# A two-layer token-mixing backbone on one core: the second layer's modulation and sums of weights loaded into slots a step ahead, and its first attention blocks placed in other slots

## The chip, the cores and the metric

The kernel runs on one core of one Trainium2 chip. The metric is the device time of one launch, in microseconds (us). Three runs of the kernel before gave 1685.3, 1686.6 and 1686.74 us; their median is 1686.6 us.

## What is computed

The reference is a backbone of two layers over 512 latent tokens (the stream X) and 256 context tokens (the stream C), 1024 channels wide. Cut to what matters here:

```python
def trunk_layer(x, ctx, c, c_ctx, ..., update_ctx):
    sh_a, sc_a, g_a, sh_f, sc_f, g_f = split(silu(c) @ w_mod + b_mod, 6)          # for x; the same with c_ctx for ctx
    zx = modulate(rms_norm(x, norm_g[0]), sh_a, sc_a) @ w_in
    zc = modulate(rms_norm(ctx, norm_g[0]), csh_a, csc_a) @ w_in
    mix_x, mix_c = token_mixers(zx, zc, ...)   # gating | mLSTM | attention | pooling, side by side
    x = x + g_a * rms_norm(mix_x @ w_out, norm_g[1])
    x = x + g_f * rms_norm(swiglu(modulate(rms_norm(x, norm_g[2]), sh_f, sc_f), w_ffn_in, w_ffn_out), norm_g[3])
    if update_ctx: ...                          # the same for ctx, in the first layer only
    return x, ctx

for l in range(2):
    x, ctx = trunk_layer(x, ctx, ..., w_mod[l], ..., update_ctx=l < 1)
return x
```

The modulation of a layer is `silu(c) @ w_mod`: a vector of 1024 times a matrix of 1024 x 6144. Everything is float32.

## The kernel before

**Products.** A float32 product is made of three TensorE matmuls of a shorter format (`mac3`, lines 491 to 493): high part times high part, low times high, high times low. Each tile of weights comes by DMA from the SP queue into a ring `wr` of seven 512 KB buffers (`weights`, L433), ACT writes its high part `wh` (L416), and DVE or POOL the low part `wl` (L417).

**Background tasks.** Each call of `weights` first calls `tick`. It adds `bg_rate` to a counter and, for each whole number that it reaches, takes a task out of the list `bg`; a second list `bg2` has a rate of its own. So work that is needed later is spread over the program of a stage. What is still in `bg` when its result is needed is issued in one go by `flush`.

**The two kinds of task of this case.** `mods_sums` makes four of the six parts of the second layer's modulation for X on DVE: 4 parts x 2 halves x 4 pairs of row blocks, 32 tasks. A task loads 512 KB of `w_mod` into one buffer of the ring `wr` (L688) and adds two scaled row blocks into an accumulator `macc` (L696 the first, L698 the others). After four tasks TensorE sums `macc` over the partitions (L704, eight small matmuls by two groups, x8 in the rows) and DVE adds the bias into `mod` (L708). `weight_sums` makes, for a Strassen form of the second layer's FFN, sums of weights: 9 tasks, each with two loads and a scratch buffer in the ring `wr`, four additions on POOL (L1566) and three stores to a DRAM tensor `ws` (L1589 to L1591). Both kinds are queued when the first layer's FFN for X begins. `bg_rate` there is 0.2, as set for an earlier stage (`rate1`).

**The first layer's end.** `layer_end` runs the output projection and then the FFN in three chunks (`fcx`); in the last one the columns are treated in two halves, so that the residual and the next norm of one half run while TensorE works on the other. In its helper the remaining tasks of `bg` are flushed (L1888 and L1891) before the second layer's projection, whose right side `hx` needs `mod`.

**Slots.** Intermediate tiles live in an `Arena` of named SBUF slots with a list of free ones, first in, first out. A tile that takes a slot waits for the last reader of what stood there.

**The second layer.** A string, `l1`, gives the order in which the pieces of the second layer's projection, mLSTM (`m`), attention (`a`), pooling (`P`) and gating (`S`) are written out; a scheduler keeps that order as the priority on every engine. `h` gives back 16 slots of `hx` after the projection; `a1` is one attention block with four heads: scores (L1115 to L1128), their exponentials into slots `pb` (L1135, the context part) and `pa` (L1140, the local part), transposes (L1162, L1168) and products. An mLSTM step ends with a norm on DVE that writes `ht` (L821), which TensorE transposes (L1452).

Of the kernel before, what the change touches and what calls it, by code (L numbers as in the profile page):

```python
# [11 lines left out]
F32 = mybir.dt.float32  # L12
# [5 lines left out]
ALU = mybir.AluOpType  # L18
# [3 lines left out]
P = 128  # L22
# [58 lines left out]
 'op1': 'P',  # L81
 'urg': 1500,
 'l0': 'k u2 q Q A B K F o u2 p2 p2 h a1 a1 S a2 a1 a2 a2 a2 P a1 a1 C N a2 R G m1',
 'l1': 'H Q R G o m2 m1 B m2 m2 m9 K u1 m2 u2 p1 p2 p2 p2 u1 u1 u1 p1 u9 p1 u1 p2 p2 p2 p2 p9 u1 h a1 m1 P a1 S a1 a1 a1 a9 a2 a1',
 'rc': 'x',
 'r0': 'x',
 'r1': 'm',
# [39 lines left out]
UNIT = 1024  # L127
# [31 lines left out]
class Arena:  # L159
# [109 lines left out]
class Build:  # L269
# [193 lines left out]
    def tick(self):  # L463
# [216 lines left out]
    def mods_sums(self, l, parts, p, streams):  # L680

        nc = self.nc
        p.mod = getattr(p, "mod", None) or self.pp.tile([P, 48, 2], F32, tag=f"mod{l}", name=f"mod{l}")

        def pair(part, i, k0, acc):
            raw = self.wr.tile([P, UNIT], F32, tag="wr", name=self.name("wr"))
            c = slice(i * 512, i * 512 + 512)
            nc.sync.dma_start(out=raw.rearrange("p (k c) -> p k c", k=2), in_=self.I["wmod"][l, part, k0:k0 + 2, :, c].rearrange("k p c -> p k c"))  # L688
            if k0 == 0:
                acc += [self.main.get("macc") for _ in range(streams)]  # L690
            for k in (k0, k0 + 1):
                w = raw[:, (k - k0) * 512:(k - k0) * 512 + 512]
                for s in range(streams):
                    t = acc[s].t[:, 0:512]
                    if k == 0:
                        nc.vector.tensor_scalar(out=t, in0=w, scalar1=self.cs[:, k, s:s + 1], scalar2=1.0, op0=ALU.mult, op1=ALU.mult)  # L696
                    else:
                        nc.vector.scalar_tensor_tensor(out=t, in0=w, scalar=self.cs[:, k, s:s + 1], in1=t, op0=ALU.mult, op1=ALU.add)  # L698
            if k0 < KT - 2:
                return  # L700
            ps = self.ms()
            for s in range(streams):
                for b in range(4):
                    nc.tensor.matmul(ps[:, s * 4 + b:s * 4 + b + 1], acc[s].t[:, b * P:(b + 1) * P], self.ones[:, 0:1], start=True, stop=True)  # L704
                acc[s].free()
            o = part * 8 + i * 4
            for s in range(streams):
                nc.vector.tensor_tensor(out=p.mod[:, o:o + 4, s], in0=ps[:, s * 4:s * 4 + 4], in1=p.bmod[:, o:o + 4], op=ALU.add)  # L708

        for part in parts:  # L710
            for i in range(2):
                acc = []
                for k0 in range(0, KT, 2):
                    self.bg.append(lambda part=part, i=i, k0=k0, acc=acc: pair(part, i, k0, acc))

    def mod_col(self, p, l, s, kind):

# [862 lines left out]
    def weight_sums(self, l, js):  # L1580

        nc = self.nc

        def task(j):
# [3 lines left out]
            v = lambda x: x.rearrange("p (a b) -> p a b", b=P)  # L1588
# [255 lines left out]
    def order(self, names, l, st, C, h, p, ring, extra):  # L1844

        x = st is not C
        self.new_mix(st)
        gens = {"m": lambda: self.mlstm(st, p, not x, not x), "u": lambda: self.in_u(l, st, h), "p": lambda: self.in_pool(l, st, h),
                "a": lambda: self.attention(st, C, p, x, ring)}
        run = {"A": lambda: self.in_rows_a(l, st, h, p), "k": lambda: self.in_k(l, st, h, p), "q": lambda: self.in_q(l, st, h, p),  # L1850
               "K": lambda: self.in_ak(l, st, h, x), "Q": lambda: self.in_aq(l, st, h, x), "B": lambda: self.in_rows_b(l, st, h, True),
               "o": lambda: self.in_o(l, st, h), "h": h.free, "S": lambda: self.sgu(st, p), "P": lambda: self.pool(st, p), "G": lambda: self.gates(st, False),
               "R": lambda: self.k_rows(st), "H": lambda: self.in_halves(l, st, h, p), "N": lambda: None, **extra}
        open_ = {}
        need = {"h": "AkqKQBoup" if "A" in names else "HKQBoup", "S": "Bu", "P": "p", "G": "A" if "A" in names else "H", "R": "k" if "A" in names else "H", "m": "GRo" + ("kq" if "A" in names else ""),
                "a": "KQB", "C": "F", "c": "F", "n": "c"}
        if not x:
            need.update(N="X", G="AX")
            assert names[0] == "A"
        ts = names.split()  # L1860
        for i, t in enumerate(ts):
            before = [x[0] for x in ts[:i]]
            assert all(x in before for x in need.get(t[0], "")), t
            if t[0] in "hS":
                assert not any(x[0] in ("up" if t[0] == "h" else "u") for x in ts[i:])
            if t[0] == "P":
                assert not any(x[0] == "p" for x in ts[i:])
        for t in ts:
            if t[0] in gens:
# [271 lines left out]
```

## Time and profile before

| | |
|---|---|
| median of three runs | 1686.6 us |
| profiled execution: device time | 1681.38 us |
| profiled execution: span of the trace | 1679.6 us |
| mean granted TensorE clock | 0.972 |
| busy share: TensorE, weight loads, DVE, ACT, POOL | 95%, 83%, 63%, 47%, 45% |
| share of the chain that ended last: TensorE, DVE | 64%, 7% |

The profile is of one execution, which took 1681.38 us; 1.8 us of it lie around the span. It is 5.2 us, or 0.3%, below the median of the three runs. Sums below are made against this execution. PE is TensorE, DVE VectorE, ACT ScalarE, POOL GpSimd, SP the engine that issues the loads.

### The profile page before, as it was taken

What the parts mean: (1) busy time and instruction counts of PE and PEld (TensorE: products, weight loads), DVE (VectorE), ACT (ScalarE), POOL (GpSimd) and SP (SyncE); (2) the same over time, 40 slices, a digit from 0 to 9 for tenths busy, and PEclk for the clock granted to TensorE, in tenths of its full rate; (3) what the DMA queues carried; (4) which work ended last, traced back from release to release, by engine and by line L of the source; (5) the groups of instructions that cost most, each with busy time, mean ns of one, the idle gap of its engine ahead of it and who ended that gap; (6) DMA issues with size and microseconds to landing.
All of it is one profiled execution on the core that took longest, in us unless ns stands there. A gap on an engine that the chain in (4) does not pass through costs nothing.

```text
span 1679.6 us, 29082 instructions
## 1 busy us (share of the span) xinstructions
PE 1596.8 (95%) x10616; PEld 1395.7 (83%) x10616; DVE 1062.5 (63%) x2312; ACT 792.8 (47%) x1782; POOL 761.4 (45%) x797
## 2 busy tenths in 40 slices
PE   6999998998999998999999997999699999999997
PEld 2976877887899897888888887999569989999996
DVE  4887676648785668532343478658774866665664
ACT  3665356654445555332332333565374545555451
POOL 2431235554466565444335324332424665564653
PEclk8999998999999999999999998999799999999998
DMA  9854563354475323445545676131031224444441
GB/s 325 271 190 160 179 201 101 123 176 142 126 247 176 117 80 124 153 155 199 180 158 171 209 249 225 40 96 64 26 93 59 95 88 132 133 138 131 126 127 58
DMA packets 94734, 245.37 MB, mean 146 GB/s; under 512 B 12032, under 2 KB 21120, under 8 KB 94592
## 3 DMA queue, kind: packets, MB, share of 16 engines
q1 hardware_dynamic: 94592, 243.52, 44.2%
q8 instruction: 83, 1.36, 0.3%
q14 instruction: 59, 0.48, 0.1%
HBM read 227.76 MB, written 15.73 MB: 145 GB/s over the span
## 4 chain that ended last, share of the span: by engine, by line
PE 64%; DVE 7%; issue 1%; DMA 1%; POOL 1%; ACT 1%; DVEq 0%; POOLq 0%; SPq 0%; ACTq 0%
PE mm L491 16%; PE mm L493 15%; PE mm L492 15%; PE mx L493 2%; PE mx L491 2%; PE mx L492 2%; PE mm L508 1%; PE mm L513 1%; PE mm L514 1%; PE mm L515 1%; PE mm L509 1%; DVE wl L417 1%; PE mm L520 1%; PE mx L1420 1%; PE mx L1168 1%
## 5 line engine op out<-in xcount | busy, mean ns | idle before, releaser
L417 POOL TENSOR_TENSOR wl<-wr,wh 128x512 fp32r<-128x512 f32 (+2 forms) x268 | 358.9, 1344 | 428.1 <-ACT wh L416 390.5
L416 ACT ACTIVATE wh<-wr 128x512 fp32r<-128x512 f32 (+3 forms) x548 | 334.9, 619 | 459.3 <-PE mm L492 340.0
L417 DVE TENSOR_TENSOR wl<-wr,wh 128x512 fp32r<-128x512 f32 (+3 forms) x280 | 220.5, 790 | 155.1 <-ACT wh L416 149.7
L491 PE MATMUL mm<-hfh_m,wh 128*128 128x512 f32 (+1 forms) x320 | 124.6, 389 | 0.0
L493 PE MATMUL mm<-hfh_m,wl 128*128 128x512 f32 (+1 forms) x320 | 124.3, 388 | 0.0
L492 PE MATMUL mm<-hfl_m,wh 128*128 128x512 f32 (+1 forms) x320 | 123.9, 387 | 0.0
L492 PE MATMUL mm<-hfl_c,wh 128*128 128x256 f32 x352 | 100.3, 285 | 0.6 <-POOL hfl_c L603 0.6
L491 PE MATMUL mm<-hfh_c,wh 128*128 128x256 f32 x352 | 100.6, 287 | 0.0
L493 PE MATMUL mm<-hfh_c,wl 128*128 128x256 f32 x352 | 99.4, 283 | 0.0
L491 PEld LDWEIGHTS mm<-hfh_c,wh 128*128 128x128 f32 x352 | 66.1, 188 | 6.6 <-issue 2.7
L493 PEld LDWEIGHTS mm<-hfh_m,wl 128*128 128x128 f32 x320 | 60.1, 188 | 13.5
L492 PEld LDWEIGHTS mm<-hfl_m,wh 128*128 128x128 f32 x320 | 60.1, 188 | 13.2
L491 PEld LDWEIGHTS mm<-hfh_m,wh 128*128 128x128 f32 x320 | 60.1, 188 | 12.9
L492 PEld LDWEIGHTS mm<-hfl_c,wh 128*128 128x128 f32 x352 | 66.4, 189 | 2.4 <-issue 1.0
L493 PEld LDWEIGHTS mm<-hfh_c,wl 128*128 128x128 f32 x352 | 66.4, 189 | 0.8 <-issue 0.4
L492 PE MATMUL mm<-gl_m,wh 128*128 128x512 f32 x152 | 59.7, 394 | 0.0
L493 PE MATMUL mm<-gh_m,wl 128*128 128x512 f32 x152 | 59.7, 394 | 0.0
L491 PE MATMUL mm<-gh_m,wh 128*128 128x512 f32 x152 | 59.6, 394 | 0.0
L698 DVE SCALAR_TENSOR_TENSOR macc_m<-wr,cs,macc_m 128x512 f32<-128x512 f32 x56 | 45.8, 836 | 18.0 <-DMA wr<-in_wmod_dram 17.6
L1566 POOL TENSOR_TENSOR wr<-wr,wr 128x512 f32<-128x512 f32 x36 | 52.8, 1479 | 1.1
L491 PE MATMUL mx<-gh_m,wh 128*128 128x512 f32 x128 | 50.9, 399 | 1.4 <-ACT wh L416 1.4
L493 PE MATMUL mx<-gh_m,wl 128*128 128x512 f32 x128 | 51.2, 400 | 1.0 <-POOL wl L417 0.6
(721 smaller groups left out, 5329.2 us busy)
## 6 DMA issues: line engine op xcount, KB each, us to landing
wr<-in_wfi_dram SPq DMA_DIRECT2D x141, 512.0 KB, 3.6
wr<-in_wmod_dram SPq DMA_DIRECT2D x80, 512.0 KB, 4.4
wr<-in_wT_dram SPq DMA_DIRECT2D x42, 512.0 KB, 4.4
wr<-in_wo_dram SPq DMA_DIRECT2D x24, 512.0 KB, 4.2
wr<-in_wfo_dram SPq DMA_DIRECT2D x24, 512.0 KB, 4.0
wr<-ws SPq DMA_DIRECT2D x18, 512.0 KB, 3.9
wm_m<-in_wmod_dram SPq DMA_DIRECT2D x32, 256.0 KB, 5.3
wr<-in_wfo_dram SPq DMA_DIRECT2D x16, 448.0 KB, 3.9
```

What stands on the lines that cost most here:

```text
L416: nc.scalar.activation(hi, src, AF.Copy)
L417: (eng or nc.vector).tensor_tensor(out=lo, in0=src, in1=hi.bitcast(F32), op=ALU.subtract)
L491: nc.tensor.matmul(out, lh, rh, start=first, stop=False, skip_group_check=more)
L492: nc.tensor.matmul(out, lh, rl, start=False, stop=False, skip_group_check=more)
L493: nc.tensor.matmul(out, ll, rh, start=False, stop=last, skip_group_check=more)
L508: nc.tensor.matmul(out, w.h[w0 + i], ah, start=f, stop=False)
L509: nc.tensor.matmul(out, w.l[w0 + i], ah, start=False, stop=False)
L513: nc.tensor.matmul(out[:, c], w.h[w0 + i], ah[:, c], start=f and q == 0, stop=False)
L514: nc.tensor.matmul(out[:, c], w.h[w0 + i], al[:, c], start=False, stop=False)
L515: nc.tensor.matmul(out[:, c], w.l[w0 + i], ah[:, c], start=False, stop=z and q == 1)
L698: nc.vector.scalar_tensor_tensor(out=t, in0=w, scalar=self.cs[:, k, s:s + 1], in1=t, op0=ALU.mult, op1=ALU.add)
L1566: tt = lambda i, o, a, b, op=ALU.subtract: self.e(engines[i]).tensor_tensor(out=o, in0=a, in1=b, op=op)
```

## The change

There are four parts. The first: `bg_rate` is set to a new value, 0.55 (`rate2`, which nothing read before), when the two kinds of task are queued. The second: a modulation task takes two slots `mw` of the Arena in place of a ring buffer, with two loads of 256 KB, and a helper `ahead` issues the loads of a task one task earlier. The third: a task of weight sums does the same with four slots `sa` and four loads of 256 KB; two more slots `sb` take sums, the operations are reordered, still four on POOL, and four stores of 256 KB take the place of three. The fourth: `l1` has brackets around the first two attention blocks and the pooling; `[` takes all free slots away from the list, so that what is written inside lives in the 16 slots that `h` gives back, and `]` puts the others back.

```diff
- 'rate2': 0.5,
+ 'rate2': 0.55,
- 'l1': 'H Q R G o m2 ... p9 u1 h a1 m1 P a1 S a1 a1 a1 a9 a2 a1',
+ 'l1': 'H Q R G o m2 ... p9 u1 [ h a1 m1 P a1 ] S a1 a1 a1 a9 a2 a1',
+    def park(self):
+        self.parked = list(self.free)
+        self.free.clear()
+    def unpark(self):
+        self.free.extend(self.parked)
+        self.parked = []
+    def ahead(self, steps):
+        box = {}
+        def start(i):
+            if i < len(steps):
+                box[i] = steps[i][0]()
+        def task(i):
+            start(i + 1)
+            steps[i][1](box.pop(i))
+        return [lambda: start(0)] + [lambda i=i: task(i) for i in range(len(steps))]
# mods_sums
-            raw = self.wr.tile([P, UNIT], F32, tag="wr", name=self.name("wr"))
+            raw = [self.main.get("mw") for _ in range(2)]
-            nc.sync.dma_start(out=raw.rearrange("p (k c) -> p k c", k=2), in_=self.I["wmod"][l, part, k0:k0 + 2, :, c].rearrange("k p c -> p k c"))
+            for k, x in enumerate(raw):
+                nc.sync.dma_start(out=x.t[:, 0:512], in_=self.I["wmod"][l, part, k0 + k, :, c])
+        self.bg.extend(self.ahead(steps))
# weight_sums
-            first, second, both = self.raw_unit(self.I["wfi"][l, j, 0]), self.raw_unit(self.I["wfi"][l, j, 1]), self.raw_unit()
-            self.form_sums(T["sap"], first, second, both)()
-            nc.sync.dma_start(out=d[:, 0], in_=v(both))
-            nc.sync.dma_start(out=d[:, 1, 0:4], in_=v(second[:, 0:512]))
-            nc.sync.dma_start(out=d[:, 1, 4:8], in_=v(first[:, 512:1024]))
+                    x = self.main.get("sa")
+                    nc.sync.dma_start(out=x.t[:, 0:512].rearrange("p (a b) -> p a b", b=P), in_=self.I["wfi"][l, j, u][:, v * 4:v * 4 + 4])
+            halves = halves + [self.main.get("sb") for _ in range(2)]
+            tt(0, s1, a21, a22, ALU.add)
+            tt(1, a21, a11, a21)
+            tt(2, s2, s1, a11)
+            tt(3, a12, a12, s2)
+            for i, x in enumerate((s2, s1, a21, a12)):
+                nc.sync.dma_start(out=d[:, i // 2, i % 2 * 4:i % 2 * 4 + 4], in_=x.rearrange("p (a b) -> p a b", b=P))
+        self.bg2.extend(self.ahead([(lambda j=j: load(j), lambda x, j=j: form(j, x)) for j in js]))
# order and mix
+            if t[0] == "[":
+                self.ar.park()
+            elif t[0] == "]":
+                self.ar.unpark()
+            self.bg_rate = T["rate2"]
```

Before the first layer's FFN for X the order of every engine is the same in both kernels. Three places show how rows move. Line numbers of the changed kernel are higher: its L442 is L433 of before, L712 stands for L688, L725 for L698, L1508 for L1477, L573 for L550, L639 for L616, L1166, L1167 and L1171 for L1135, L1136 and L1140.

**SP at the end of the first layer's FFN.** `in_wfo` are the last weights of the FFN, `in_wT` the first ones of the second layer's projection. Before, the first rows of a run of 20 loads of `w_mod` behind the last weights of the FFN:

```order
L433 DMA wr_11087<-in_wfo_dram 128x896
L433 DMA wr_11097<-in_wfo_dram 128x896
L433 DMA wr_11107<-in_wfo_dram 128x896
L688 DMA wr_11455<-in_wmod_dram 128x2x512
L688 DMA wr_11460<-in_wmod_dram 128x2x512
L688 DMA wr_11464<-in_wmod_dram 128x2x512
L688 DMA wr_11468<-in_wmod_dram 128x2x512
```

and the end of that run:

```order
L688 DMA wr_11556<-in_wmod_dram 128x2x512
L688 DMA wr_11560<-in_wmod_dram 128x2x512
L433 DMA wr_11661<-in_wT_dram 128x1024
L433 DMA wr_11671<-in_wT_dram 128x1024
L433 DMA wr_11681<-in_wT_dram 128x1024
L433 DMA wr_11691<-in_wT_dram 128x1024
```

In the changed kernel the same place has (`mw` the slots of the modulation, `sa` those of the sums of weights):

```order
L442 DMA wr_11320<-in_wfo_dram 128x896
L442 DMA wr_11330<-in_wfo_dram 128x896
L442 DMA wr_11340<-in_wfo_dram 128x896
L1620 DMA sa_m_11093<-in_wfi_dram 128x512
L442 DMA wr_11779<-in_wT_dram 128x1024
L442 DMA wr_11789<-in_wT_dram 128x1024
L712 DMA mw_m_11285<-in_wmod_dram 128x512
L712 DMA mw_m_11286<-in_wmod_dram 128x512
L442 DMA wr_11799<-in_wT_dram 128x1024
L442 DMA wr_11809<-in_wT_dram 128x1024
```

The 20 loads have gone up the queue, among the FFN's weights, and the projection's weights stand right behind the FFN's; three loads of 256 KB are left there.

**DVE at the same place.** `y` is the FFN's output, added up chunk by chunk; `sq` are squares for its norm, `rs` the first half's residual. Before:

```order
L1477 TENSOR_TENSOR y_m_9174<-mm_11296,y_m_9174 128x256
L698 SCALAR_TENSOR_TENSOR macc_m_11526<-wr_11533,cs,macc_m_11526 128x512
L698 SCALAR_TENSOR_TENSOR macc_m_11549<-wr_11556,cs,macc_m_11549 128x512
L698 SCALAR_TENSOR_TENSOR macc_m_11526<-wr_11533,cs,macc_m_11526 128x512
L616 SCALAR_TENSOR_TENSOR rs_t_11435<-y_m_9171,Gf_8263,mx_11432 128x256
L616 SCALAR_TENSOR_TENSOR rs_t_11435<-y_m_9172,Gf_8263,mx_11432 128x256
```

and behind the first half's residual:

```order
L698 SCALAR_TENSOR_TENSOR macc_m_11549<-wr_11556,cs,macc_m_11549 128x512
L1477 TENSOR_TENSOR y_m_9175<-mm_11321,y_m_9175 128x256
L698 SCALAR_TENSOR_TENSOR macc_m_11526<-wr_11537,cs,macc_m_11526 128x512
L617 TENSOR_TENSOR x_m_7444<-x_m_7444,rs_t_11440 128x256
L617 TENSOR_TENSOR x_m_7446<-x_m_7446,rs_t_11445 128x256
L1477 TENSOR_TENSOR y_m_9176<-mm_11347,y_m_9176 128x256
L617 TENSOR_TENSOR x_m_7448<-x_m_7448,rs_t_11450 128x256
L724 SCALAR_TENSOR_TENSOR Af_14159<-mod_4493,ng_4471 128x8
L698 SCALAR_TENSOR_TENSOR macc_m_11549<-wr_11560,cs,macc_m_11549 128x512
L1477 TENSOR_TENSOR y_m_9177<-mm_11372,y_m_9177 128x256
```

In the changed kernel:

```order
L1508 TENSOR_TENSOR y_m_9194<-mm_11503,y_m_9194 128x256
L573 TENSOR_TENSOR sq_m_11222<-sq_m_11222,sq_e_11526 128x256
L605 TENSOR_SCALAR rmsv_11661<-ms_11656 128x2
L1508 TENSOR_TENSOR y_m_9195<-mm_11529,y_m_9195 128x256
L639 SCALAR_TENSOR_TENSOR rs_t_11668<-y_m_9192,Gf_8263,mx_11665 128x256
L639 SCALAR_TENSOR_TENSOR rs_t_11668<-y_m_9193,Gf_8263,mx_11665 128x256
```

and behind the residual:

```order
L1508 TENSOR_TENSOR y_m_9196<-mm_11554,y_m_9196 128x256
L640 TENSOR_TENSOR x_m_7444<-x_m_7444,rs_t_11673 128x256
L640 TENSOR_TENSOR x_m_7446<-x_m_7446,rs_t_11678 128x256
L1508 TENSOR_TENSOR y_m_9197<-mm_11580,y_m_9197 128x256
L640 TENSOR_TENSOR x_m_7448<-x_m_7448,rs_t_11683 128x256
L426 TENSOR_TENSOR wt_m_11786<-wr_11779,wt_m_11785 128x512
L573 TENSOR_TENSOR sq_m_11222<-sq_m_11222,sq_e_11577 128x256
L426 TENSOR_TENSOR wt_m_11792<-wr_11789,wt_m_11791 128x512
L1508 TENSOR_TENSOR y_m_9198<-mm_11605,y_m_9198 128x256
```

The additions into `macc` are gone from between the steps of the norm and the residual; the last three of them (L725) stand before the FFN's last half.

**ACT and PE at the second layer's first attention block.** `mxs` is a row's maximum, `mix1h` the high part of an mLSTM step's result. ACT before:

```order
L1136 ACTIVATE mxs_13564<-sink_4483,mxs_13564 128x1
L1136 ACTIVATE mxs_13583<-sink_4483,mxs_13583 128x1
L1135 ACTIVATE pb_m_13559,mxs_13564<-mm_13561,mxs_13564 128x256
L1135 ACTIVATE pb_m_13559,mxs_13583<-mm_13580,mxs_13583 128x256
L416 ACTIVATE mix1h_m_13082<-o_m_12524 128x128
L416 ACTIVATE mix1h_m_13084<-o_m_12525 128x128
L1136 ACTIVATE mxs_13602<-sink_4483,mxs_13602 128x1
L1140 ACTIVATE pa_m_13612,mxs_13602<-mm_13604,mxs_13602 128x256
L1140 ACTIVATE pa_m_13593,mxs_13583<-mm_13585,mxs_13583 128x256
```

ACT in the changed kernel:

```order
L1166 ACTIVATE pb_m_13677,mxs_13682<-mm_13679,mxs_13682 128x256
L1167 ACTIVATE mxs_13682<-sink_4483,mxs_13682 128x1
L1171 ACTIVATE pa_m_13692,mxs_13682<-mm_13684,mxs_13682 128x256
L1166 ACTIVATE pb_m_13677,mxs_13701<-mm_13698,mxs_13701 128x256
L1167 ACTIVATE mxs_13701<-sink_4483,mxs_13701 128x1
L1171 ACTIVATE pa_m_13711,mxs_13701<-mm_13703,mxs_13701 128x256
L319 ACTIVATE pb_m_13677<-pb_m_13677,mxs_13682 128x256
```

All exponentials of the block now stand ahead of the next `mix1h`. On PE, before, `L1452` takes the last mLSTM step, and the scores of the second block (`mm_13728`, `mm_13733`) stand around it:

```order
L1115 MATMUL mm_13728<-ak_c_8007,aq_m_12190 128x256
L1116 MATMUL mm_13728<-ak_c_8007,aq_m_12190 128x256
L1452 MATMUL mx_13212<-ident,ht_m_13151 128x128 x2
L1123 MATMUL mm_13733<-ak_m_13221,aq_m_12190 128x384
L1124 MATMUL mm_13733<-ak_m_13222,aq_m_12190 128x384
```

In the changed kernel the last step (L1483) has the second block's scores above it, and directly behind it come the transposes of `pb` (L1193, which was L1162):

```order
L1454 MATMUL mx_13299<-C_1231_8636,qi_m_12628 128x130
L1454 MATMUL mx_13299<-C_1231_8636,qi_m_12629 128x130
L1483 MATMUL mx_13290<-ident,ht_m_13269 128x128
L1483 MATMUL mx_13330<-ident,ht_m_13269 128x128
L1193 MATMUL mx_13756<-ident,pb_m_13677 128x128 x4
L1193 MATMUL mx_13763<-ident,pb_m_13678 128x128 x4
```

## Rows read from the trace of the kernel before

**Rows 1.** Windows by stage: length, then each engine's busy us, PE clock, DMA share, GB/s.

```profile
680.00:990.00 310.00, 310.00 (x1415) 253.09 (x1414) 123.90 (x178) 101.10 (x174) 130.09 (x109) 1.00 0.53 177
990.00:1080.00 90.00, 80.18 (x582) 77.62 (x581) 71.19 (x136) 31.66 (x74) 38.80 (x54) 0.89 0.55 191
1160.00:1240.00 80.00, 63.45 (x454) 51.53 (x454) 65.19 (x234) 42.11 (x122) 26.71 (x38) 0.85 0.09 28
```

**Rows 2.** Timeline of PE: start, us, operation, idle before it and its releaser.

```profile
1029.08 0.95 PE L704 MATMUL ms<-ones,macc_m 128*128 128x1 f32 x8
...
1031.28 0.28 PE L493 MATMUL mm<-gh_m,wt_m 128*128 128x256 f32 x1
1036.87 1.87 PE L704 MATMUL ms<-ones,macc_m 128*128 128x1 f32 x8 [5.32 <-DVE mod L708]
...
1044.57 1.87 PE L704 MATMUL ms<-ones,macc_m 128*128 128x1 f32 x8 [1.91 <-DVE mod L708]
1046.69 1.87 PE L575 MATMUL ms<-ones,sq_t 128*128 128x1 f32 x8 [0.25 <-DVE mod L708]
...
1052.92 0.58 PE L508 MATMUL mm<-hxh_m,wt_m 128*128 128x256 f32 x1
```

**Rows 3.** Timeline of DVE in the same gap.

```profile
1034.84 1.90 DVE L698 SCALAR_TENSOR_TENSOR macc_m<-wr,cs,macc_m 128x512 f32<-128x512 f32 x1
...
1039.32 0.41 DVE L1477 TENSOR_TENSOR y_m<-mm,y_m 128x256 f32<-128x256 f32 x1
```

**Rows 4.** Timeline of SP's queue: start, us until the last issue, count.

```profile
975.91 41.11 SPq L688 DMA_DIRECT2D wr<-in_wmod_dram  x20
1017.32 6.51 SPq L433 DMA_DIRECT2D wr<-in_wT_dram  x4
```

**Rows 5.** DVE's costliest group from 985 to 1050 us: count, busy us, mean ns.

```profile
L698 DVE SCALAR_TENSOR_TENSOR macc_m<-wr,cs,macc_m 128x512 f32<-128x512 f32 x35 | 27.0, 801 | 0.1
```

**Rows 6.** Timeline of PE at the next join, before the second layer's FFN.

```profile
1303.35 0.50 PE L575 MATMUL ms<-ones,sq_m 128*128 128x1 f32 x4
...
1306.10 0.39 PE L508 MATMUL mm<-hf00h_m,wt_m 128*128 128x256 f32 x1 [1.18 <-ACT hf00h_m L598]
```

**Rows 7.** DVE's group of modulation sums from 680 to 990 us.

```profile
L698 DVE SCALAR_TENSOR_TENSOR macc_m<-wr,cs,macc_m 128x512 f32<-128x512 f32 x21 | 18.3, 871 | 17.9 <-DMA wr<-in_wmod_dram 17.6
```

**Rows 8.** A wait of SP's queue from 680 to 990 us: total, times, longest.

```profile
SPq L1590 <- POOL wr L1566: 39.6, 9, 7.0
```

**Rows 9.** DMA issues from 680 to 990 us: count, KB each, us to landing.

```profile
wr<-in_wmod_dram SPq DMA_DIRECT2D x17, 512.0 KB, 4.6
ws<-wr SPq DMA_DIRECT2D x18, 256.0 KB, 3.6
```

**Rows 10.** Waits of PE from 1160 to 1240 us.

```profile
PE mx L1452 <- DVE ht_m L821: 8.1, 3, 3.0
PE mm L1115 <- ACT pa_m L1140: 5.2, 2, 3.3
```

**Rows 11.** Timeline of ACT, an exponential of the first attention block.

```profile
1200.66 0.47 ACT L1140 ACTIVATE pa_m<-mm,mxs 128x256 f32<-128x256 f32 x1 [4.25 <-DVE ht_m L821]
```

**Rows 12.** Timeline of DVE between two mLSTM steps.

```profile
1193.57 1.59 DVE L1086 SCALAR_TENSOR_TENSOR pd_m<-s_m,pinv,pz_m 64x512 f32<-64x512 f32 x1
...
1196.57 0.75 DVE L1086 SCALAR_TENSOR_TENSOR pd_m<-s_m,pinv,pz_m 64x512 f32<-64x512 f32 x1
```

**Rows 13.** Timeline of PE from the first scores to the first transposes.

```profile
1184.27 0.28 PE L1115 MATMUL mm<-ak_c,aq_m 128*128 128x256 f32 x1
...
1188.70 0.33 PE L1452 MATMUL mx<-ident,ht_m 128*128 128x128 f32 x1 [2.56 <-DVE ht_m L821]
...
1200.24 0.47 PE L1452 MATMUL mx<-ident,ht_m 128*128 128x128 f32 x1 [2.98 <-DVE ht_m L821]
...
1209.34 0.92 PE L1452 MATMUL mx<-ident,ht_m 128*128 128x128 f32 x2 [2.58 <-DVE ht_m L821]
...
1212.84 1.43 PE L1162 MATMUL mx<-ident,pb_m 128*128 128x128 f32 x8
```

More of the change, by code (lines that the diff above doesn't have):

```diff
@@ L83 @@
  'l0': 'k u2 q Q A B K F o u2 p2 p2 h a1 a1 S a2 a1 a2 a2 a2 P a1 a1 C N a2 R G m1',
- 'l1': 'H Q R G o m2 m1 B m2 m2 m9 K u1 m2 u2 p1 p2 p2 p2 u1 u1 u1 p1 u9 p1 u1 p2 p2 p2 p2 p9 u1 h a1 m1 P a1 S a1 a1 a1 a9 a2 a1',
+ 'l1': 'H Q R G o m2 m1 B m2 m2 m9 K u1 m2 u2 p1 p2 p2 p2 u1 u1 u1 p1 u9 p1 u1 p2 p2 p2 p2 p9 u1 [ h a1 m1 P a1 ] S a1 a1 a1 a9 a2 a1',
  'rc': 'x',
@@ L683, in mods_sums, with load, pair @@
         p.mod = getattr(p, "mod", None) or self.pp.tile([P, 48, 2], F32, tag=f"mod{l}", name=f"mod{l}")
-        def pair(part, i, k0, acc):
-            raw = self.wr.tile([P, UNIT], F32, tag="wr", name=self.name("wr"))
+        def load(part, i, k0):
+            raw = [self.main.get("mw") for _ in range(2)]
             c = slice(i * 512, i * 512 + 512)
-            nc.sync.dma_start(out=raw.rearrange("p (k c) -> p k c", k=2), in_=self.I["wmod"][l, part, k0:k0 + 2, :, c].rearrange("k p c -> p k c"))
+            for k, x in enumerate(raw):
+                nc.sync.dma_start(out=x.t[:, 0:512], in_=self.I["wmod"][l, part, k0 + k, :, c])
+            return raw
+        def pair(part, i, k0, acc, raw):
             if k0 == 0:
@@ L691, in pair @@
             for k in (k0, k0 + 1):
-                w = raw[:, (k - k0) * 512:(k - k0) * 512 + 512]
+                w = raw[k - k0].t[:, 0:512]
                 for s in range(streams):
@@ L698, in pair @@
                         nc.vector.scalar_tensor_tensor(out=t, in0=w, scalar=self.cs[:, k, s:s + 1], in1=t, op0=ALU.mult, op1=ALU.add)
+            for x in raw:
+                x.free()
             if k0 < KT - 2:
@@ L708, in pair @@
                 nc.vector.tensor_tensor(out=p.mod[:, o:o + 4, s], in0=ps[:, s * 4:s * 4 + 4], in1=p.bmod[:, o:o + 4], op=ALU.add)
+        steps = []
         for part in parts:
@@ L713, in mods_sums @@
                 for k0 in range(0, KT, 2):
-                    self.bg.append(lambda part=part, i=i, k0=k0, acc=acc: pair(part, i, k0, acc))
+                    steps.append((lambda part=part, i=i, k0=k0: load(part, i, k0), lambda x, part=part, i=i, k0=k0, acc=acc: pair(part, i, k0, acc, x)))
+        self.bg.extend(self.ahead(steps))
     def mod_col(self, p, l, s, kind):
@@ L1582, in weight_sums, with load, form @@
         nc = self.nc
-        def task(j):
-            first, second, both = self.raw_unit(self.I["wfi"][l, j, 0]), self.raw_unit(self.I["wfi"][l, j, 1]), self.raw_unit()
-            self.form_sums(T["sap"], first, second, both)()
-            d = self.sums[l, j] = self.dr.tile([P, 2, KT, P], F32, tag=f"ws{l}{j}", name=f"ws{l}{j}")
-            v = lambda x: x.rearrange("p (a b) -> p a b", b=P)
-            nc.sync.dma_start(out=d[:, 0], in_=v(both))
-            nc.sync.dma_start(out=d[:, 1, 0:4], in_=v(second[:, 0:512]))
-            nc.sync.dma_start(out=d[:, 1, 4:8], in_=v(first[:, 512:1024]))
-        self.bg2.extend(lambda j=j: task(j) for j in js)
+        def load(j):
+            halves = []
+            for u in range(2):
+                for v in range(2):
+                    x = self.main.get("sa")
+                    nc.sync.dma_start(out=x.t[:, 0:512].rearrange("p (a b) -> p a b", b=P), in_=self.I["wfi"][l, j, u][:, v * 4:v * 4 + 4])
+                    halves.append(x)
+            return halves
+        def form(j, halves):
+            halves = halves + [self.main.get("sb") for _ in range(2)]
+            a11, a12, a21, a22, s1, s2 = (x.t[:, 0:512] for x in halves)
+            tt = lambda i, o, a, b, op=ALU.subtract: self.e(T["sap"][i]).tensor_tensor(out=o, in0=a, in1=b, op=op)
+            tt(0, s1, a21, a22, ALU.add)
+            tt(1, a21, a11, a21)
+            tt(2, s2, s1, a11)
+            tt(3, a12, a12, s2)
+            d = self.sums[l, j] = self.dr.tile([P, 2, KT, P], F32, tag=f"ws{l}{j}", name=f"ws{l}{j}")
+            for i, x in enumerate((s2, s1, a21, a12)):
+                nc.sync.dma_start(out=d[:, i // 2, i % 2 * 4:i % 2 * 4 + 4], in_=x.rearrange("p (a b) -> p a b", b=P))
+            for x in halves:
+                x.free()
+        self.bg2.extend(self.ahead([(lambda j=j: load(j), lambda x, j=j: form(j, x)) for j in js]))
     def strassen_pair(self, l, j, h, rhs, g, jj):
@@ L1868, in order @@
         for t in ts:
-            if t[0] in gens:
+            if t[0] == "[":
+                self.ar.park()
+            elif t[0] == "]":
+                self.ar.unpark()
+            elif t[0] in gens:
                 for _ in range(int(t[1])):
```

## Prediction

> **What bounds the kernel now.** TensorE (PE) is busy for 95% of the span, so I first looked for the stages in which it isn't. I cut the span into stages by the windows view, then read the waits of PE in the two stages with gaps, then the timelines of PE and of the engine that it waits for. Where the first layer's FFN for X runs, from 680 to 990 us, PE is busy for all 310.00 us at the full clock, while DVE has 123.90 and POOL 130.09 [rows 1]: nothing can be won there, and DVE has 186 us to spare. From 990 to 1080 us PE lacks 9.8 us and from 1160 to 1240 us 16.6, both with a lower granted clock [rows 1]. These two places are the ones that the change touches.
>
> The first is the end of that FFN. Its last matmul starts at 1031.28; then PE stands until three groups of the modulation's small matmuls come, each after a wait for DVE (5.32 us the first, 1.91 the third, and one of about 2 between), and the projection's first matmul runs at 1052.92 [rows 2]. DVE is the one that is late: 35 additions into `macc` of 801 ns mean lie between 985 and 1050 us, 27.0 us in all [rows 5], and they stand in front of the FFN's own last steps: the addition of the FFN's last output `y` comes at 1039.32, some 7.8 us after the matmul that made it had ended [rows 2, 3]. The cause lies in the queues: at a rate of 0.2 a task per tile of weights, 12 of the 32 tasks are taken in the FFN, and the other 20 are issued as one run of loads that lasts from 975.91 to 1017 us, with the projection's weights behind them [rows 4].
>
> The second place is the second layer's first attention. PE waits 8.1 us there for an mLSTM step's norm (`ht`) and 5.2 us for exponentials `pa` [rows 10]. An exponential of `pa` in its turn waits 4.25 us for `ht` on DVE [rows 11], which it doesn't read: the slot that it writes was last used by the mLSTM.
>
> **Edit 1, the rate, with edit 2, the loads of modulation.** At 0.55 the 20 tasks of the run go into the FFN. What it takes away: the gap of 1052.92 − 1031.56 = 21.4 us [rows 2] shrinks to the chain which the FFN's end and the next norm need anyway: `y` added, squared and summed (about 1.2 us, from 0.41 us of such an addition in rows 3, three such steps), eight small matmuls, the root, the spreading matmuls, the product with the norm. From the sums of squares to the projection these took 1052.92 − 1046.69 = 6.2 us at the lower clock [rows 2]; at the next join, with half the tokens, 1306.10 − 1303.35 = 2.75 us [rows 6]. So the gap that stays is between 1.2 + 2.75 = 4.0 and 1.2 + 6.2 = 7.4 us. I take 6, since this join has eight matmuls where that one has four, but at a higher clock than 1046.69 had. The gap gives back 21.4 − 6 = 15.4.
>
> What it adds: the three late groups of `L704` now run inside a stage in which PE is full. At the full clock one group takes 0.95 us [rows 2], so 3 × 0.95 = 2.9 us go back. Net 12.5, with 11 to 14.5 as its ends; 9 if a last `mod` still comes late. Part of the gap before runs at the lower of PE's two levels, 1.2 GHz (a group takes 1.87 us where 0.95 is the full clock's time [rows 2]); I count nothing for a clock that may come back earlier, as a gap of 6 us may lower it too.
>
> DVE gets some 40 more additions in the FFN. There the mean of one is 871 ns [rows 7], so 35 us, on 123.90 of 310. The cover is DVE's slack of 186 us; without it each microsecond of DVE would be one of PE, because DVE writes `wl` for half the tiles. One burst can still delay a `wl`: a task has two or three additions, 2.6 us at most, and PE uses a tile (12 matmuls at 310/1415 = 0.22 us [rows 1]) in 2.6 us, with five tiles in the ring. I take nothing, and 3 us of loss as the far end.
>
> The loads become 256 KB pieces in slots outside the ring. The 17 loads of 512 KB landed in 4.6 us, 18 transfers of 256 KB the other way in 3.6 [rows 9], so two halves issued together, a whole task ahead, are no later than one. The share of DMA time in the FFN is 0.53 [rows 1]; 20 more loads of 0.5 MB on the 54.8 MB that 177 GB/s make in 310 us raise it to about 0.63. A rule of the Trainium skill speaks against the split: "SBUF — State Buffer", section "The DMA setup-cost knee", says that a transfer pays a roughly fixed cost near 2 us whatever its size, and asks to coalesce. By its fit a 256 KB piece takes an estimated 2.6 us and a 512 KB one 3.2, so if pieces queued one behind another the 32 tasks would pay 32 × 2.0 us more. The rows here agree with the shape (half the bytes, 78% of the time). As the pieces overlap and lie ahead of their use, the sum has nothing for it.
>
> **Edit 3, sums of weights.** Four additions on POOL as before, 36 in all, so POOL's time stays; 59 more rows on SP. In the FFN SP's queue waits 39.6 us for POOL's sums alone [rows 8], and PE doesn't wait once: this edit lengthens a lead that nobody used. Taken as 0; it may lose what the 3 us above hold.
>
> **Edit 4, the slots.** In the order of the changed kernel all four heads' exponentials stand ahead of the next `mix1h` on ACT, and both scores of block two ahead of the last mLSTM step on PE. Before, the steps on PE start at 1188.70, 1200.24 and 1209.34, and the transposes of `pb` at 1212.84 [rows 13]. In the first interval, 11.5 us, DVE also does 1.59 + 0.75 us of the pooling's `pd` [rows 12], which now stands later: the second step comes at about 1198, the third at 1207, and the transposes right behind it at 1208, 4.8 us earlier. The `pd` work, with what goes with it some 3 us, moves into a stretch behind the transposes in which DVE is nearly full; it costs 0 to 3, and I take 0.8, because PE has block one's products there. Gain 4. The ends: +9 if block one's transposes also leave the steps behind (1208 less another 4), −3 if all of the `pd` work is paid and block two, which must take block one's slots, waits for them.
>
> **Sum.** 12.5 + 4 − 0.5 (for a late `wl`) = 16. The profiled execution goes from 1681.4 to 1665.4, and its median of runs, 5.2 us above it, from 1686.6 to 1670.6; I say 1671.
>
> **The rivals.** *The slots lose* (0.13): only 16 slots are open to two blocks and the pooling, so block two waits for block one's transposes. For it: the transposes still stand behind the last mLSTM step. Against: 8.1 us of the waits there are the steps' own [rows 10]. Then 12.5 − 3 or a little less, 1676 to 1681.
>
> *The gap stays half* (0.08): the half that is normed last, its chain of small steps at the lower clock, keeps 11 to 13 us of the 21.4; gain 6 + 4, so 1676 to 1678.
>
> *The FFN starves, slower* (0.04): SP's queue is in order. A load into `mw` or `sa` waits for the last reader of its slot, which can be a PE matmul of an older tile, and all the weights' loads stand behind it. It decides from 16/32 = 0.5 us of PE per task on; at 1 us per task the loss is 32 − 16, so 1703. Against it: waits of up to 7.0 us on that queue [rows 8] now cost PE nothing.
>
> *No effect* (0.05): the run of additions merely moves, because a late load delays the tasks, and DVE is again late at 1031; then 1684 to 1688.
>
> **Numbers.** The forecast has 0.70. The likeliest time is 1671; the range goes from 1662 (14.5 + 9) to 1681, the far end of the first two rivals, and leaves out the last two cases and some of the tail. A measurement of this kernel can tell about 0.2%, 3.4 us, from no change. Faster holds the forecast and the first two rivals, 0.91; same 0.05; slower 0.04.
>
> **What would show it.** After the change PE should have no wait for `mod` in front of the small matmuls, a gap of 4 to 7.4 us between the FFN's last matmul and the projection's first, still 310 of 310 busy in the FFN, and DVE some 35 us more there. The stretch from the first scores to the transposes of `pb` should shrink from 28.6 us to about 24, and no exponential wait for `ht`. PE waits for `wl` in the FFN, or a first gap above 11 us, would make the prediction wrong.

## The result and the profile after

The changed kernel is slower. Its median is 1695.51 us (four runs, 1691.81 to 1698.37) against 1685.95 us before (four runs, 1684.64 to 1686.74); the ratio is 1.0053, with a 95% interval from 1.0037 to 1.0069. The forecast was 1671 us.

The profiled execution has a span of 1693.5 us, 13.9 more than the one of before, which was itself a quick one (4.6 us under the median). The windows of the same stages, to be laid beside [rows 1] (length, then busy us of TensorE, weight loads, DVE, ACT, POOL, then the granted clock, the DMA share and GB/s):

```profile
680.00:990.00 310.00, 306.48 (x1405) 251.30 (x1404) 157.86 (x206) 90.61 (x155) 127.47 (x102) 0.98 0.61 193
990.00:1080.00 90.00, 79.59 (x530) 73.62 (x529) 57.74 (x97) 35.38 (x80) 45.82 (x56) 0.92 0.43 133
1160.00:1240.00 80.00, 62.47 (x439) 53.12 (x438) 61.26 (x231) 39.14 (x107) 27.23 (x37) 0.84 0.10 33
```

DVE has 34 us more in the FFN, and the DMA share there is 0.61; the forecast was some 35 us and about 0.63. But TensorE now misses 3.5 us there and the clock falls to 0.98. So time was lost in the stage that had none to lose. The same event in both traces shows where (times in us; the lag is what the changed kernel is behind):

| event | before | after | lag |
|---|---|---|---|
| a gate of the FFN's first chunk (`ft` on ACT) | 683.42 | 686.80 | 3.4 |
| the third gate after it | 708.78 | 718.34 | 9.6 |
| a gate late in the FFN | 949.56 | 962.73 | 13.2 |
| the FFN's last matmul | 1031.28 | 1049.37 | 18.1 |
| the projection's first matmul with `hx` | 1052.92 | 1061.94 | 9.0 |
| first scores of the second layer | 1184.27 | 1193.44 | 9.2 |
| transposes of `pb`, block one | 1212.84 | 1218.01 | 5.2 |
| transposes of `pb`, block two | 1223.82 | 1238.64 | 14.8 |
| end of the span | 1679.6 | 1693.5 | 13.9 |

The first 3.4 us are not counted as a loss. The run with the brackets alone (below) has the program of before in this stage, and it reaches the same gate at 687.69, later still: executions differ by that much. The change itself loses 14.7 us in the FFN (6.2 up to the third gate, 3.6 up to the late one, 4.9 behind it), gives back 9.1 at its end and 4.0 up to block one, and loses 9.6 in block two. Of the 3.6 us, 2.9 are the three groups of small matmuls that the forecast counted.

**The loss in the FFN.** TensorE's only wait from 680 to 1000 us is this one:

```profile
PE mx L1381 <- DVE C L1390: 3.5, 1, 3.5
```

L1381 and L1390 belong to the context's mLSTM state, whose last steps overlap with the start of the FFN. The timelines of DVE, POOL and PE at that place (start, us, instruction, and in brackets the idle time before it):

```profile
702.71 6.70 DVE L725 SCALAR_TENSOR_TENSOR macc_m<-mw_m,cs,macc_m 128x512 f32<-128x512 f32 x1
709.34 1.23 DVE L1390 COPY C<-mx 64x130 f32<-64x130 f32 x4
```

```profile
702.63 1.29 POOL L1627 TENSOR_TENSOR sa_m<-sa_m,sa_m 128x512 f32<-128x512 f32 x1
703.88 1.30 POOL L1627 TENSOR_TENSOR sb_m<-sb_m,sa_m 128x512 f32<-128x512 f32 x1
705.14 1.28 POOL L426 TENSOR_TENSOR wl<-wr,wh 128x512 fp32r<-128x512 f32 x1
706.39 1.26 POOL L1627 TENSOR_TENSOR sa_m<-sa_m,sb_m 128x512 f32<-128x512 f32 x1
707.61 1.26 POOL L426 TENSOR_TENSOR wl<-wr,wh 128x512 fp32r<-128x512 f32 x1
```

```profile
706.17 0.40 PE L514 MATMUL mm<-hfh_m,wh 128*128 128x512 f32 x1
710.09 0.70 PE L1381 MATMUL mx<-vaug_c,kw_c 128*64 128x65 f32 x8 [3.52 <-DVE C L1390]
...
711.31 0.63 PE L516 MATMUL mm<-hfh_m,wl 128*128 128x512 f32 x1
```

One addition of the modulation takes 6.70 us, from the start of a run of five POOL instructions without a gap to just behind its end; the median of the 56 additions is 0.75. The state's copy stands behind it on DVE, TensorE waits for that copy, and the matmuls after it take 0.63 us where 0.40 is the full clock's time, until 715.6. In two other runs with both kinds of slots the same addition took 6.71 and 7.00 us.

At the FFN's end, where 4.9 us are lost, there is a second meeting. POOL runs seven instructions from 999.10 to 1009.66 with no gap of note, the four sums of a task among them, and DVE's low parts (L426) beside them take some 1.65 us each where one takes 0.55 by itself (998.72). TensorE then waits for `gl` and for `macc`, and after the second wait its matmuls take 0.41 us in place of 0.28 until 1026.4:

```profile
1000.47 3.33 DVE L426 TENSOR_TENSOR wt_m<-wr,wt_m 128x384 fp32r<-128x384 f32 x2 [0.25 <-ACT wt_m L425]
1008.44 1.77 DVE L429 SCALAR_TENSOR_TENSOR gl_m<-ft_m,gh_m 128x512 fp32r<-128x512 f32 x1
1010.27 0.50 PE L515 MATMUL mm<-gl_m,wh 128*128 128x512 f32 x1 [1.04 <-DVE gl_m L429]
1020.97 1.02 PE L733 MATMUL ms<-ones,macc_m 128*128 128x1 f32 x8 [2.33 <-DVE macc_m L725]
```

The two kinds of task also meet in their slots. From 680 to 1000 us SP's queue holds loads of the modulation (L712) back until stores of the sums have left a slot, and at the FFN's end it issues the last of these loads only at 1010.24 (at 995.4 in the run with slots for the modulation alone):

```profile
SPq L712 <- DMA ws<-sa_m: 17.3, 10, 3.5
SPq L712 <- DMA ws<-sb_m: 5.8, 3, 2.5
```

No run tells what these waits add to what the late DVE costs.

**The join.** The lines that answer to [rows 2]:

```profile
1049.37 0.28 PE L516 MATMUL mm<-gh_m,wt_m 128*128 128x256 f32 x1
1055.18 1.84 PE L598 MATMUL ms<-ones,sq_t 128*128 128x1 f32 x8 [5.54 <-DVE sq_t L573]
1057.83 1.87 PE L598 MATMUL ms<-ones,sq_m 128*128 128x1 f32 x8 [0.81 <-DVE rmsv L605]
1059.56 2.46 PE L609 MATMUL mx<-ident,rmsy 128*128 128x128 f32 x8
1061.94 0.58 PE L531 MATMUL mm<-hxh_m,wt_m 128*128 128x256 f32 x1
```

The wait for `mod` is gone from here, and the gap is 12.3 us in place of 21.4, not 6. TensorE waits for the squares `sq_t` of the first half.

**The attention.** From the first scores to block one's transposes it takes 24.6 us where it took 28.6; the forecast said about 24. But the pooling (L1098 on POOL) now waits for those transposes, which it did not before:

```profile
1223.79 1.47 POOL L1098 TENSOR_TENSOR s_m<-pz_m 128x526 f32<-128x526 f32 x1 [1.98 <-PE mx L1193]
```

### The profile page after: what moved, and what is told of

Same layout as the page of the kernel before. It is cut to its first block, busy times and chain, and to the rows that moved or that the text cites. A ratio compares the mean times of both kernels' runs of the same rounds, so it can differ in the third digit from the quotient of the medians.

```text
span 1693.5 us, 29258 instructions
## 1 busy us (share of the span) xinstructions
PE 1607.3 (95%) x10616; PEld 1404.1 (83%) x10616; DVE 1084.2 (64%) x2312; ACT 792.0 (47%) x1782; POOL 768.7 (45%) x797
## 4 chain that ended last, share of the span: by engine, by line
PE 79%; DVE 11%; DMA 4%; issue 3%; POOL 1%; ACT 1%; SPq 0%; DVEq 0%; POOLq 0%; ACTq 0%
PE mm L514 19%; PE mm L515 18%; PE mm L516 18%; PE mx L516 2%; PE ms L678 2%; PE mx L514 2%; PE mx L515 2%; PE mx L1199 2%; DVE wl L426 1%; PE mx L1193 1%; DMA ws<-sa_m 1%; PE mx L1451 1%; PE mm L536 1%; PE mm L537 1%; PE mm L538 1%
## 5 line engine op out<-in xcount | busy, mean ns | idle before, releaser
L426 POOL TENSOR_TENSOR wl<-wr,wh 128x512 fp32r<-128x512 f32 (+2 forms) x268 | 362.0, 1356 | 441.9 <-ACT wh L425 401.3
L426 DVE TENSOR_TENSOR wl<-wr,wh 128x512 fp32r<-128x512 f32 (+3 forms) x280 | 226.5, 812 | 144.9 <-ACT wh L425 141.8
L725 DVE SCALAR_TENSOR_TENSOR macc_m<-mw_m,cs,macc_m 128x512 f32<-128x512 f32 x56 | 62.6, 1119 | 23.1 <-DMA mw_m<-in_wmod_dram 22.2
L515 PE MATMUL mx<-gl_m,wh 128*128 128x512 f32 x128 | 50.9, 398 | 0.0
```

What stands on the lines that cost most here:

```text
L426: (eng or nc.vector).tensor_tensor(out=lo, in0=src, in1=hi.bitcast(F32), op=ALU.subtract)
L515: nc.tensor.matmul(out, lh, rl, start=False, stop=False, skip_group_check=more)
```

## The experiments

All ratios are to the kernel before, in runs on the same chip. Its own median there lay between 1686.27 and 1687.37 us, so across experiments the ratios are compared, not the times.

**One part at a time.** The rate alone:

```diff
             self.mods_sums(1, (2, 4, 3, 5), pn, 1)
+            self.bg_rate = T["rate2"]        # 0.55, loads in the ring
```

> The kernel before with the rate of 0.55 alone: loads of the modulation stay in the ring, no sums in slots, no brackets. Theory A (the tasks hurt wherever they stand in DVE's order in the FFN, since they are stretched beside POOL and stand in front of what TensorE waits for): the loss in the FFN stays and the gap at its end shrinks by about 9, so 1686 to 1694 us. Theory B (the new loads and the four sums in a row on POOL do the harm): the tasks of the ring cost the 3 us of their small matmuls and little else, and the gap gives back 9 to 15, so 1674 to 1680 us.

Measured: 1684.53 us, ratio 0.9982 (0.9971 to 0.9993). The median lies between the two ranges, nearer to theory A's, and yet TensorE has no wait from 680 to 1000 us. In its trace the lag grows by 3.9 us within the FFN (three groups of small matmuls, 2.9, and 1 more) and falls by 9.1 at the join, where the gap is 12.3 us as in the changed kernel. The rate is a small gain; it isn't what made the kernel slower.

The brackets alone (`u1 [ h a1 m1 P a1 ] S` in the kernel before):

> The kernel before with the brackets in the second layer's order alone. Theory A (the brackets gain 4 us up to the first block's transposes and lose 9 to 10 in the second block and the pooling): 1690 to 1692 us. Rival (what the trace of the changed kernel lost there came from the clock or from other state, not from the slots): 1682 to 1687 us.

Measured: 1691.68 us, ratio 1.0024 (1.0015 to 1.0033), in theory A's range: they lose 4 us. Block one's transposes come 24.6 us after the first scores and block two's 46.0, much as in the changed kernel (24.6 and 45.2; 28.6 and 39.5 before).

The changed kernel without them (`u1 h a1 m1 P a1 S`):

> The changed kernel without the brackets. Theory A (the brackets lose 5 us net): 1689 to 1692 us. Rival (the brackets are neutral or gain): 1694 to 1700 us.

Measured: 1693.53 us, ratio 1.0038 (1.0025 to 1.0051). The median is 2 us under that of the changed kernel and lies between the two ranges; the rest of the loss, 6 us, stays without brackets. It has the long addition too (6.71 us at 706.50) and the wait of 3.6 us.

The bracket around block one alone (`[ h a1 ] m1 P a1`):

> The changed kernel with the closing bracket behind the first attention block, so that the pooling and the second block can take other slots once those that block one left are used. If the second block's wait for the first one's transposes is what loses 9 to 10 us, some of it comes back and the first 4 us stay: 1684 to 1690 us. If it is the pooling's work that was moved behind, or if the second block still meets the slots of the mLSTM: 1691 to 1697 us.

Measured: 1698.02 us, ratio 1.0067 (1.0053 to 1.0080): no better, and above both ranges. It has the long addition as well (7.00 us). When the bracket closes, two of the 16 slots are unused; behind them in the list come the ones that block one frees, and only then the others. The pooling still takes block one's, and in the trace it still waits for block one's transposes (1.46 us of idle time on POOL). So it told only that moving the bracket isn't enough.

**The two kinds of slots.** Rate and modulation slots, with the sums of weights in the ring as before (`weight_sums` of the kernel before):

> The changed kernel without the brackets and with the sums of weights in the ring as before: rate and modulation slots alone. The rate alone measured 0.18% faster, rate with both kinds of slots 0.38% slower: 9 us between them. If POOL's four sums in a row, which stretch a DVE addition from 0.75 to 6.7 us in front of what TensorE waits for, make the 9 us: 1684 to 1687 us, no wait of TensorE for the state copies, no addition above 2 us. If the modulation's early loads and their place in SP's queue make it: 1690 to 1694 us.

Measured: 1680.65 us, ratio 0.9963 (0.9950 to 0.9975), better than either range; no addition above 1.81 us, no wait of TensorE from 680 to 1000 us.

Rate and slots for the sums, with the modulation in the ring (`mods_sums` of the kernel before):

> The changed kernel without the brackets and with the modulation in the ring: rate and slots for the sums of weights alone. If POOL's four sums in a row do the harm: 1688 to 1694 us, with DVE additions of several us in the FFN. If the modulation's slots do it: 1683 to 1687 us.

Measured: 1682.49 us, ratio 0.9975 (0.9965 to 0.9985), just under the second range. My theory that the sums in a row alone do the harm fell: no addition above 1.80 us. With the rate (0.9982 alone), neither kind of slot does harm by itself: slots for the modulation seem a small gain, and those for the sums can't be told from none. Both together turn 0.9963 and 0.9975 into 1.0038. The harm lies in their meeting.

Two ways to keep them apart. The modulation begins behind the state's copies:

```diff
+ 'rate2': 0.67,
             self.bg_rate = T["rate2"]
+            self.bg_acc = -6.0
```

> The changed kernel without the brackets, with the first modulation task put off by six tasks and a rate of 0.67 to make up for it, so that no addition stands ahead of the state copies of the context on DVE. If TensorE's wait for those copies with the slow clock behind it is worth 6 us of the 9: 1686 to 1689 us, with the wait gone. If such a stretch only moves to another place where TensorE waits for DVE: 1692 to 1695 us.

Measured: 1686.49 us, ratio 0.9997 (0.9987 to 1.0007), as the first theory said: 7 us faster than without the delay, and both the wait for the copies and the long addition are gone (the longest takes 1.89 us). But other waits come up in its trace: TensorE waits 2.3 us for a low part `wl` of POOL, at 971 us, and 0.7 for `gl` at the FFN's end, where DVE's low parts take 1.6 us beside POOL's run.

The sums on DVE:

```diff
- 'sap': 'PPPP',
+ 'sap': 'VVVV',
```

> The changed kernel without the brackets, with the four sums of a task on DVE in place of POOL. If it is POOL's sums in a row that hold up DVE's additions: additions of 2 us or less, no wait for the state copies, and 25 us more DVE in the FFN, under its spare time: 1685 to 1689 us. If DVE's own load is what delays the low parts: 1693 to 1700 us, with more waits for DVE in the FFN.

Measured: 1683.97 us, ratio 0.9986 (0.9977 to 0.9996), a little under the first range and about 9 us faster than the same with POOL, although DVE does 36 more additions. DVE's timeline at the same place; here the state's copies come in two parts with one addition between them:

```profile
704.12 0.61 DVE L1390 COPY C<-mx 64x130 f32<-64x130 f32 x2
...
705.36 1.70 DVE L725 SCALAR_TENSOR_TENSOR macc_m<-mw_m,cs,macc_m 128x512 f32<-128x512 f32 x1
706.98 0.58 DVE L1390 COPY C<-mx 64x130 f32<-64x130 f32 x2
```

**The slots of the attention.** On rate and modulation slots, the bracket around block one, and a turned list behind it, in which the six slots that the mLSTM uses last stand at the end:

```diff
-        self.free.extend(self.parked)
+        done = list(self.free)
+        self.free.clear()
+        self.free.extend(done[:2] + self.parked[6:] + done[2:] + self.parked[:6])
```

> Rate and modulation slots (the run above that measured 0.37% faster), with the bracket around the first attention block alone, and at its end a list of free slots in which the slots that the mLSTM uses last come behind all others, so that the pooling no longer takes slots of block one. Theory (the first block's 4 us are real, and what the brackets lose comes from the pooling's wait for block one's transposes): the transposes come 24 to 25 us after the first scores, the second block's are not late, and the whole gains 3 to 5 us on that run: 1675 to 1679 us. Rival (the second block is held back by something else, such as its place behind the last mLSTM steps): no gain or a loss, 1680 to 1688 us.

Measured: 1682.60 us, ratio 0.9972 (0.9963 to 0.9982): no gain on 0.9963, and in the rival's range. DVE and PE between the first scores and block one's transposes:

```profile
1191.34 1.65 DVE L1119 SCALAR_TENSOR_TENSOR pd_m<-s_m,pinv,pz_m 64x512 f32<-64x512 f32 x2 [0.31 <-PE mx L1453]
...
1207.26 1.75 DVE L1119 SCALAR_TENSOR_TENSOR pd_m<-s_m,pinv,pz_m 64x512 f32<-64x512 f32 x1
```

```profile
1183.77 0.28 PE L1148 MATMUL mm<-ak_c,aq_m 128*128 128x256 f32 x1
...
1213.73 0.48 PE L1485 MATMUL mx<-ident,ht_m 128*128 128x128 f32 x1 [1.86 <-DVE ht_m L854]
1214.00 1.92 PE L1195 MATMUL mx<-ident,pb_m 128*128 128x128 f32 x8
```

The pooling's `pd` work is back between the mLSTM steps, and the first transposes come after 30.2 us, not 24.6, although block one has the same slots as in the changed kernel. Block two's come 42.0 us after the first scores (at 1225.74), where it takes 39.5 us in the kernel before and 45.2 in the changed one. So the 4 us don't seem to be won from the slots: they go with the pooling's work, which the brackets put off.

**The join.** The additions of squares of every norm on DVE (`'sqk': 'VVVVVVVV'` for `'VPVPVPVP'`), on rate and modulation slots:

> Rate and modulation slots, with the seven additions of squares of each norm on DVE alone in place of DVE and POOL by turns. Theory (the gap of 12 us at the first layer's end is the chain of the first half's residual and squares, in which DVE and POOL stretch each other and wait for each other): the gap shrinks by 2 to 4 us, to about 9, and the whole gains as much, 1676 to 1679 us. Rival (DVE is full there and takes the additions' time itself): the gap stays at 12 or grows, 1680 to 1686 us.

Measured: 1672.30 us, ratio 0.9919 (0.9906 to 0.9933), the fastest here, but not for the reason given: the gap at the join is 11.8 us (from 1031.59 to 1043.42) in place of 12.3. Against the profile without this edit it is 8.7 us ahead at 886 us already, before the join, and its FFN is as long (the table below). The gain comes ahead of the FFN, where the norms' sums are: the three profiles with this edit reach the gate of the first row above at 680.8 to 682.7 us, the eleven without it at 683.4 to 690.5, with a median of 688.3. The same edit on the kernel before:

> The kernel before with the additions of squares of each norm on DVE alone, nothing else. If the 8 us that this edit gave on top of rate and modulation slots come from the norms ahead of the first layer's FFN, where the program is that of before, it gives 7 to 9 us here too: 1677 to 1680 us. If it needs DVE to be free of the late modulation at the first layer's end: 1684 to 1688 us.

Measured: 1682.14 us, ratio 0.9971 (0.9959 to 0.9983), between the two ranges. So some 5 us of it don't need the other edits; whether the rest does is open.

The residual's additions on DVE too (`'rsk': 'VVVVVVVV'` for `'PPVPVPVP'`):

> Rate, modulation slots and squares on DVE (0.81% faster in its run), with the residual's additions on DVE alone too, in place of POOL for five of eight. If the gap of 12 us at the first layer's end is the first half's chain from its norm over residual and squares to the next norm, shortening the residual by some 2 us shortens the gap as much: a gap of 9 to 10.5 us, 1668 to 1671 us. If DVE is what fills that chain: the gap stays at 12 us or grows, 1672 to 1676 us.

Measured: 1681.93 us, ratio 0.9966 (0.9953 to 0.9978), 8 us worse than without it and above both ranges. The lines of the join:

```profile
1041.53 1.84 PE L598 MATMUL ms<-ones,sq_t 128*128 128x1 f32 x8 [8.35 <-DVE sq_t L573]
...
1047.66 0.58 PE L531 MATMUL mm<-hxh_m,wt_m 128*128 128x256 f32 x1
```

The last matmul ended at 1033.19, so the gap grew to 14.5 us, and the wait for `sq_t` from 5.6 to 8.4. DVE's own work fills this chain: giving it more made it longer. That is 2.6 of the 8 us; the edit changes the residual of every norm, and where the rest lies the runs don't show.

## Why the prediction was wrong

The sum was 12.5 for the modulation, 4 for the slots of the attention and 0.5 lost; the measured change is 9.6 us the other way. Step by step:

- **That the late modulation holds up the join, and that it goes away** was right: no matmul there waits for `mod` (L737) any more.
- **The gap that stays** was the first step that failed: "between 1.2 + 2.75 = 4.0 and 1.2 + 6.2 = 7.4 us. I take 6", where it is 12.3 in all nine kernels with the higher rate and the norms as before, and 11.8 and 14.5 in the two with more of the norms on DVE. I let the chain begin at the FFN's last matmul. It begins earlier, at the norm of the first half: with rate and modulation slots, L609 runs at 1031.91 and TensorE can sum `sq_t` at 1045.87, 14 us later, and on DVE the residual (L639, L640), the squares (L573) and two low parts of the projection's weights (L426) share that time. The two matmuls, and DVE's timeline between them:

```profile
1031.91 0.61 PE L609 MATMUL mx<-ident,rmsy 128*128 128x128 f32 x4
1045.87 1.84 PE L598 MATMUL ms<-ones,sq_t 128*128 128x1 f32 x8 [5.56 <-DVE sq_t L573]
```

```profile
1032.55 3.22 DVE L639 SCALAR_TENSOR_TENSOR rs_t<-y_m,Gf,mx 128x256 f32<-128x256 f32 x8 [2.12 <-PE mx L609]
1035.69 0.42 DVE L1508 TENSOR_TENSOR y_m<-mm,y_m 128x256 f32<-128x256 f32 x1
1036.02 1.82 DVE L640 TENSOR_TENSOR x_m<-x_m,rs_t 128x256 f32<-128x256 f32 x2
...
1038.65 1.23 DVE L426 TENSOR_TENSOR wt_m<-wr,wt_m 128x512 fp32r<-128x512 f32 x1
1039.80 0.96 DVE L573 TENSOR_TENSOR sq_m<-sq_m,sq_e 128x256 f32<-128x256 f32 x1
1040.69 1.21 DVE L426 TENSOR_TENSOR wt_m<-wr,wt_m 128x512 fp32r<-128x512 f32 x1
...
1043.56 2.16 DVE L573 TENSOR_TENSOR sq_t<-sq_t,sq_t 128x256 f32<-128x256 f32 x2
```

  It is busy from 1032.55 on without a pause. The run with the residual on DVE supports this: there the same stretch is 17.0 us. So the rate, counted as 15.4 given back less 2.9, gives 9.1 less 3.9 in the trace of the rate alone, and 3 us in its runs. One of the rivals had this size: *the gap stays half* says 11 to 13 us. It put it down to small steps at the lower clock. They are there, 6.8 us from the sums of the squares to the projection, near the 6.2 that the forecast read; what neither has is the wait of 5.5 us for the first half's squares ahead of them.
- **What the additions cost in the FFN** ("I take nothing, and 3 us of loss as the far end") and **the sums of weights** ("Taken as 0") are the step that turned the sign. I summed the work of each engine and found it covered, and priced the edits apart. Together they put an addition, a run of POOL's sums and the state's copies next to each other. The stage's length shows what each edit does to it: from the gate of the table's first row to the FFN's last matmul. Profiles whose program is the same there, but for the squares, agree within 1 us (347.8 to 347.9 in three, 350.5 in three, 362.6 to 363.6 in three):

| kernel | FFN, us | ratio in its runs |
|---|---|---|
| before | 347.9 | 1 |
| rate alone | 351.7 | 0.9982 |
| rate, slots for the modulation | 350.5 | 0.9963 |
| rate, slots for the sums | 352.5 | 0.9975 |
| rate, both kinds, no brackets | 363.6 | 1.0038 |
| the changed kernel | 362.6 | 1.0053 |
| no brackets, modulation delayed | 356.5 | 0.9997 |
| no brackets, sums on DVE | 354.4 | 0.9986 |

  Both kinds cost 13.0 us more than the modulation's alone, and that is the whole difference in the runs (0.75%, 12.6 us): 6.0 by the third gate, at the state's copies, and 7.0 behind the late gate, at the FFN's end; between them nothing. The delay takes back 7.1 and the sums on DVE 9.1, in the runs 7 and 9. What is left, 6.0 and 3.9 us, is in this stage too. Whether POOL's runs beside DVE or the loads that wait for the sums' stores make it, no run separates.
- **The slots of the attention**: the mechanism was right up to the first transposes (24.6 us, forecast about 24), and the mis-sized term is the pooling's work, "0 to 3, and I take 0.8". Block two lost 9.6 us: the pooling waited for block one's transposes, and its products stand on TensorE just ahead of block two's transposes (with 1.4 us of wait for `pd`). How the 9.6 us divide between that, the other short waits there and the lower clock was not separated. The rival that the slots lose was the right one for this edit, and its price was near: it took 3 us lost where the forecast had 4 gained, and the brackets alone lose 4.
- **The rival with the other sign** pointed at the right stage and the wrong mechanism: it had SP's queue starve the FFN of weights. No wait of TensorE for a load shows there; SP's queue did hold back loads of the modulation for the sums' stores, as shown above, but it is the late addition that TensorE waits for. That it has the right sign is luck.

The split of the loads into 256 KB pieces, against which the Trainium skill ("SBUF — State Buffer", "The DMA setup-cost knee") speaks, did no harm that can be seen: the kernel with the modulation in such pieces is 0.37% faster than before, and 0.19% better than the one with the rate alone (the two intervals overlap a little).

The lower end of the range, 1662, is not quite its own sum: 1686.6 less 14.5 and 9 is 1663.1. Nothing hangs on it.

## What to carry to other kernels

A sum of work per engine doesn't price work that is put into a stage where TensorE is full: look instead at what stands next in the queue behind each added instruction, and who waits for that. Two edits that do no harm one by one can lose together, so test each edit alone and also leave each one out of the whole. Compare the length of a stage between two landmarks inside it rather than the time at which it begins. And when a wait is taken away, trace the next chain from where it starts, which can lie well before the last matmul, and through the engine that does its work.

## What the runs showed of the hardware that was not expected

A DVE addition with two SBUF inputs (0.75 us by itself) was held for a whole run of POOL instructions rather than one: 6.70 us beside five of 1.3 us without a gap, and 6.71 and 7.00 us in two more kernels with the same order. Most other meetings cost less: the long two-input instructions of the FFN in these traces are near 1.8 us, the longest beside these three 3.3 us, and at the FFN's end of the changed kernel each of DVE's took about as long as one of POOL's (some 1.65 us), although POOL's seven had hardly a gap either. What decides between the two isn't shown. The Trainium skill ("GPSIMD Engine Reference", section "1. Specifications") says that POOL shares its SBUF interfaces with VectorE and that they contend when a DVE instruction has two SBUF inputs; the trace agrees, and adds how long it can last.

Executions differ more in where this FFN begins than in how long it takes. Ten kernels whose program is that of before up to there, and the kernel before itself, reached a gate at its start between 652.0 and 657.9 us; the length behind the gate at 683 us repeated within 1 us (the table above). So one profile is no measure for a change of a few us in the time at which something happens, but here it was one for the length of this stage.
